# First stage over half of the rows for two sets of seven column tiles

## The chip, the cores and the metric

One core of one Trainium2 chip runs the kernel. The metric is device time in microseconds, the median of several runs. The engines are TensorE (matrix products into PSUM), VectorE, ScalarE, GpSimd and SyncE, which here issues every DMA. Each has its own queue of instructions; the kernel writes them in an order of its own (a manual schedule), and semaphores hold an instruction until its inputs and its buffer are ready. [...]

## The reference, cut to what matters

A layer over 512 latent tokens and 256 context tokens, 2048 wide:

```python
mod = silu(c) @ w_ada + b_ada            # c for latent, c_ctx for context; thirds: shift, scale, gate
h   = rmsnorm(x) * (1 + scale) + shift   # latent and context
b, c, u, g, v, q = split(h @ w_in)       # six parts of 1024 columns, 48 column tiles of 128
ya  = b * conv3(c * u) * silu(g)         # latent only
xb  = conv4(v) + bias                    # latent and context
for d in (forward, backward):            # RG-LRU, 16 heads of 64 channels
    r, i = sigmoid(xb @ wa + ba), sigmoid(xb @ wx + bx)
    a    = exp(-8 r softplus(-lam));  bt = sqrt(1 - a*a) * (i * xb)
    y   += linear_scan(a, bt)            # starts from the context's last state
yb  = y * silu(q)
out = rmsnorm(x + gate * (concat(ya, yb) @ w_out)) * final_g
```

## The kernel before, in words

Everything is fp32. A product is made of three passes in a reduced fp32 form (`mm3`, lines 77 to 80): the weights and the activations are each split into a high and a low part, and high by high, low by high and high by low are summed in one PSUM bank. So each weight tile of 128x1024 is loaded as `raw`, cast by ScalarE to `whi` (line 73), and VectorE makes `wlo` from the difference (line 74). Five `raw` buffers and three each of `whi` and `wlo` turn round. The activations lie transposed, 16 row tiles of 128 features by 512 tokens.

*Head.* The 16 tiles of x are loaded, squared and summed over the features by a product with ones into one of four column strips of the array (lines 208 to 219). From the ninth on each is followed by a product of ones with ones that nothing reads. The sums are gathered, an inverse root is made with one Newton step, transposed, and copied to all partitions (`rinvB`).

*Ada.* For each of the 16 row tiles g, shift and scale of latent and context are products of silu(c) and silu(c_ctx) with `w_ada`. `ada(g, p)` multiplies a quarter p of the rows: four products at a time in four column strips of 32. The weights come in four DMAs of 512 KB to eight buffers `rada`. After p = 3 ScalarE copies the sums (`sada`, line 205), two transposes and a few small VectorE instructions (`ada_t`, `mods`, lines 239 to 244) turn them into scale and shift, and `h_lat(g)` makes the activations: `xhi` on VectorE (line 247), its high part on ScalarE (248), the low part `hlo` on VectorE (249).

*First stage* (`main_a`). For each row tile k in turn, seven column tiles (A_TILES) are multiplied into seven banks, with the weights `wa_` of 448 KB a row tile. Between them stand, in this order: after tile 0 the split of the next row's weights (`split_a(k+1)`) and the second half of ada(k+1); after tile 1 `ada_t(k+1)` and `h_lat(k+1)`; after tile 5 the first half of ada(k+2). In k = 0 a softplus of 24 small VectorE instructions (`softplus`) follows `h_lat(1)`. The context tiles are loaded in the last two row tiles, squared by ScalarE after them and summed by GpSimd (`ctx_sq`).

*Steps.* The other 41 column tiles take two steps each, one for each half of the 16 row tiles, 24 products a step, with one weight piece of 512 KB a step, loaded three steps and split two steps ahead (`load_piece`, `split_piece`). BC_TILES sets the order: three tiles, the eight v tiles, which multiply the 256 context tokens too, the rest of c, u, b and g, and the eight q tiles. At the end of a step stands the evaluation (`EV`) of the tile that ended in the step before it, and then what the table `bg` says for the step; `mid` is issued between the fourth and the fifth row tile. The tables hold: the context's norm and activations (`ctx_stat`, `ctx_stat2`, `h_ctx`, steps 2 to 5); the gate third of ada as a sum on VectorE, one weight row of 512 KB every second step (`gt_load`, `gt_acc`), and at its end four sums over partitions (`gt_sum`); and from step S_C0 = 22 on the RG-LRU, one head tile m of 128 channels every seven steps. With b its first step: split of its weights and of xb (`l_prep`) at b, four gates (`l_gate`) in the middles of b+2 to b+5, tanh and exp (`l_exp`) at b+5, GpSimd and VectorE products (`l_mul`) at b+6, square roots (`l_sqrt`) at b+7, the scans (`l_scan`) at b+8. All gates use one pair of banks, which ScalarE's two sigmoids (`lr`, `li`, lines 460 and 461) free. `lr` and `li` have two buffers each, one a direction, which the scan of the head tile before still uses.

*Output.* 32 steps: four groups of 512 output columns by eight pieces of `w_out`. Each piece is multiplied with the gate first (VectorE, line 316) and then split; TensorE sums into four banks, one for each 128 tokens; `d_ev` adds x, squares and sums. The last pieces are reordered so that the final norm of each 128 tokens can start early.

Of the kernel before, what the change touches and what calls it, by code (L numbers as in the profile page):

```python
# [14 lines left out]
D = 2048  # L15
KT = D // 128
T = 512
# [12 lines left out]
for _n, _w in PCOLS:  # L30
# [5 lines left out]
A_TILES = [("c", 0), ("u", 0), ("b", 0), ("g", 0), ("c", 1), ("u", 1), ("b", 1)]  # L36
_REST = [("g", 1)] + [(n, m) for m in range(2, NM) for n in "cubg"]
N_FIRST = 3
BC_TILES = (_REST[:N_FIRST] + [("v", m) for m in range(NM)] + _REST[N_FIRST:]
            + [("q", m) for m in range(NM)])  # L40
NA = len(A_TILES)
W_OFF = {"b": 0, "c": 8, "u": 16, "g": 24, "v": 32, "q": 40}
N_BC = 2 * len(BC_TILES)
# [6 lines left out]
def tile_hybrid_layer(ctx, tc, xt, ct, xn, wada, wgt, bgt, wa_, wbc, wout, lruw, par, ident, fg, out):  # L50
# [11 lines left out]
    ctx.enter_context(tc.manual_schedule())  # L62
    s_a = ExitStack()
    ta = s_a.enter_context(tc.tile_pool(name="ta", bufs=2))
    pa = ctx.enter_context(tc.tile_pool(name="pa", bufs=6, space=PSUM))
# [96 lines left out]
    aux = pa.tile([128, 512], F32, name="bacc")  # L162
    acc = [pa.tile([128, 512], F32, name="bacc") for i in range(NA - 2)]
    accp = pa.tile([128, 2, 512], F32, name="plru", bufs=1)
    acc += [accp[:, 0, :], accp[:, 1, :]]
# [22 lines left out]
    for p in range(4):  # L188
        load_ada(0, p)
    load_wa(0)  # L190
    for p in range(4):
        load_ada(1, p)
    load_wa(1)

# [4 lines left out]
    def ada(g, p):  # L199
        for j in range(4):  # L200
            nc.tensor.matmul(aux[32 * j:32 * j + 32, 0:256], cs[:, 4 * p + j, :], rawa[g, p][:, j, :],  # L201
                             start=p == 0, stop=p == 3, skip_group_check=True)
        if p == 3:
            st = ta.tile([128, 256], F32, name="sada")
            nc.scalar.copy(st, aux[:, 0:256])
            rawa["s", g] = st
# [12 lines left out]
    ssum = ta.tile([128, T], F32, name="sq", bufs=4)  # L219
# [7 lines left out]
    ada(0, 0)  # L227
    ada(0, 1)
# [4 lines left out]
    ada(0, 2)  # L233
    ada(0, 3)

    def ada_t(g):
        st = rawa["s", g]
        for h in range(2):
            nc.tensor.transpose(aux[:, 256 + 128 * h:384 + 128 * h], st[:, 128 * h:128 * h + 128], idt)
        m = ta.tile([128, 2, 2], F32, name="mods")  # L240
        v = aux[:, 256:512].rearrange("p (s q v) -> p s v q", s=2, q=4)[:, :, 0:2, :]
        nc.vector.tensor_reduce(m, v, axis=AX.X, op=ALU.add)  # L242
        nc.vector.tensor_scalar(gs[:, g, :], m[:, 0, :], bsc1[:, g:g + 1], pc("ng", g), op0=ALU.add, op1=ALU.mult)
        nc.vector.tensor_scalar(sh[:, g, :], m[:, 1, :], pc("bsh", g), None, op0=ALU.add)
# [13 lines left out]
    def h_ctx(ks):  # L258
        for k in ks:
            nc.vector.scalar_tensor_tensor(xc[k], xc[k], gs[:, k, 1:2], cq["b"], op0=ALU.mult, op1=ALU.mult)  # L260
        for k in ks:
            hctx[k] = (hc.tile([128, TC], F32R, name="xchi", bufs=16 + NHC), hc.tile([128, TC], F32R, name="hclo"))
            nc.scalar.activation(hctx[k][0], xc[k], AF.Identity, bias=sh[:, k, 1:2])
        for k in ks:
# [3 lines left out]
    def ctx_sq(k):  # L268
        t = ta.tile([128, TC], F32, name="sqc", bufs=12) if k else const.tile([128, TC], F32, name="sqc0")
# [6 lines left out]
    def ctx_stat():  # L276
        ps = pa.tile([128, 512], F32, name="bacc")
# [7 lines left out]
    def ctx_stat2():  # L285
        ps = pa.tile([128, 512], F32, name="bacc")
# [5 lines left out]
    def main_a(k, j):  # L292
        hi, lo = wsp["a", k]
        s = slice(128 * j, 128 * j + 128)
        mm3(acc[j], hi[:, s], lo[:, s], hlat[k], T, k == 0, k == KT - 1)


    def piece_src(s):
        if s < N_BC:
            return wbc[s]  # L300
        return wout[s - N_BC]

# [7 lines left out]
    def split_piece(s):  # L310
        raw = rawq.pop(s)
        if s >= N_BC:
            c = (s - N_BC) // 8
# [5 lines left out]
    ada_t(0)  # L319
    h_lat(0)  # L320
    split_a(0)
    ada(1, 0)
    ada(1, 1)
    for k in range(KT):
        if k + 2 < KT:
            for p in range(4):
                load_ada(k + 2, p)
            load_wa(k + 2)
        else:
            load_piece(k + 2 - KT)  # L330
            for kk in range(8 * (k - 14), 8 * (k - 14) + 8):
                load_xc(kk)
        main_a(k, 0)
        if k + 1 < KT:
            split_a(k + 1)
            ada(k + 1, 2)
            ada(k + 1, 3)
        else:
            split_piece(0)
        main_a(k, 1)  # L340
        if k + 1 < KT:
            ada_t(k + 1)
# [12 lines left out]
    s_a.close()


    yp = ctx.enter_context(tc.tile_pool(name="yp", bufs=8, reuse_waits="tile"))
    gp = ctx.enter_context(tc.tile_pool(name="gp", bufs=1, reuse_waits="tile"))
    s_c = ExitStack()  # L360
    tq = [s_c.enter_context(tc.tile_pool(name="tcx", bufs=1, reuse_waits="tile"))]
    s_l = ExitStack()
    lp = [None]
    gacc = gp.tile([128, D], F32, name="gacc")
    nc.gpsimd.memset(gacc, 0.0)
# [12 lines left out]
    def ev_u(m, ps):  # L378
        cu = tq[0].tile([128, T], F32, name="cutile")
        nc.vector.tensor_tensor(cu, cur["c"], ps, op=ALU.mult)  # L380
        y = yp.tile([128, T], F32, name="yA")
# [30 lines left out]
    def ev_v(m, ps, psc):  # L412
        t = yp.tile([128, TA], F32, name="xb")
# [31 lines left out]
    def l_gate(m, d, h):  # L445
# [5 lines left out]
        ps = pa.tile([128, 2, 512], F32, name="plru", bufs=1)  # L451
        pf = ps.rearrange("p a b -> p (a b)")
# [53 lines left out]
    def gt_sum(j):  # L506
        p = pa.tile([128, 512], F32, name="bacc")
        s = slice(512 * j, 512 * j + 512)
        nc.tensor.matmul(p, ones, gacc[:, s], start=True, stop=True)
        nc.scalar.copy(gacc[:, s], p)  # L510
        gq[0] = gacc

    S_C0 = 2 * (N_FIRST + NM)
    bg, mid = {}, {}

    def at(step, f, *args, q=bg):
        q.setdefault(step, []).append((f, args))


    for m in range(NM):  # L520
        b = S_C0 + 7 * m
        if m:
            at(b, l_sqrt, m - 1)
        at(b, l_prep, m)
        if m:
            at(b + 1, l_scan, m - 1)
# [8 lines left out]
    at(S_C0 + 7 * NM, l_sqrt, NM - 1)  # L535
    at(S_C0 + 7 * NM + 1, l_scan, NM - 1)
    for i in range(N_GT):
        at(3 + 2 * i, gt_load, i)
        at(4 + 2 * i, gt_acc, i)
    for j in range(4):  # L540
        at(3 + 2 * N_GT + j, gt_sum, j)
    at(1, lambda: nc.sync.dma_start(gacc[0:1, :], bgt))
    at(2, ctx_stat)
    at(3, ctx_stat2)
    at(3, h_ctx, range(0, 3))
    at(4, h_ctx, range(3, 6))
    at(4, h_ctx, range(6, 9))
    at(5, h_ctx, range(9, 12))
    at(5, h_ctx, range(12, 15))
    at(5, h_ctx, range(15, 16))  # L550


    S_Y = S_C0 + 7 * NM + 2
# [8 lines left out]
    for k in range(6):  # L562
        at(S_Y + k // 3, lambda k=k: y_split(dp1[0], k))
# [230 lines left out]
```

## Time and profile before

| | us |
|---|---|
| median of 3 runs (857.98 to 859.2) | 858.03 |
| the profiled execution's own time | 858.19 |
| its span, first to last instruction | 856.4 |
| TensorE busy, of the span | 838.6 (98%) |
| VectorE, ScalarE, GpSimd busy | 493.5, 376.6, 89.1 |
| the 16th row tile of the first stage starts; the last of its products starts | 146.38; 150.91 |
| spacing of products in a step there | 0.227, so 24 take 5.45 |
| a v step (24 products of 512 and 24 of 256 columns) | 8.3 |
| VectorE: split of a piece; one gate row; gate on a piece of w_out | 1.25; 1.33; 1.30 |
| VectorE: the convolutions of one v tile | 4.8 |
| bytes moved, mean rate | 136.13 MB, 159 GB/s |

The profile is that of one execution. A busy TensorE says little, since its products are pipelined and the ends of the records are modelled: the spacing of starts counts. What matters is who waits: the chain of waits follows the execution back from its end, and the list of waits says which instruction an engine stood before and which other one released it. Lines are those of the kernel before.

### The profile page before, as it was taken

How to read it: one execution, taken by the hardware profiler on the slowest of the kernel's cores; microseconds unless marked ns; L12 is line 12 of the kernel's file. 1: busy time of each engine (PE TensorE's matmuls, PEld its weight loads, DVE VectorE, ACT ScalarE, POOL GpSimd, SP SyncE). 2: the span in 40 equal slices, each digit the busy share in tenths (PEclk: the TensorE clock that was granted, in tenths of full speed). 3: DMA queues.
4: the chain of work that ended last, by engine and by line, in shares of the span. 5: the costliest groups of instructions: out<-in, count | busy, mean ns of one | idle time of the engine just before them, and what ended most of it. 6: DMA issues, size and time to landing. Idle time of an engine off the chain costs nothing.

```text
span 856.4 us, 10577 instructions
## 1 busy us (share of the span) xinstructions
PE 838.6 (98%) x4202; PEld 665.3 (78%) x4202; DVE 493.5 (58%) x643; ACT 376.6 (44%) x478; POOL 89.1 (10%) x64
## 2 busy tenths in 40 slices
PE   7899999999999999999999999999999999999996
PEld 1466666888888888878888888887788888888784
DVE  0353434786355446394939585766465777454555
ACT  6322224451111024757576857475846443222234
POOL 0000001600000000202020202120202002020200
PEclk9899999999999999999999999999999999999998
DMA  9899998234222324244435443434223542323204
GB/s 341 341 326 333 352 357 291 103 120 139 82 99 82 116 86 159 99 131 152 143 116 164 145 159 122 161 123 135 74 99 141 204 171 102 120 74 113 84 0 197
DMA packets 41091, 136.13 MB, mean 159 GB/s; under 512 B 4561, under 2 KB 6865, under 8 KB 40401
## 3 DMA queue, kind: packets, MB, share of 16 engines
q1 hardware_dynamic: 41042, 135.46, 44.8%
q8 instruction: 33, 0.54, 0.3%
q14 instruction: 16, 0.13, 0.0%
HBM read 131.24 MB, written 4.19 MB: 158 GB/s over the span
## 4 chain that ended last, share of the span: by engine, by line
PE 93%; DVE 3%; ACT 1%; DMA 1%; issue 1%; SPq 0%; POOL 0%; ACTq 0%; DVEq 0%; POOLq 0%
PE bacc L78 21%; PE bacc L79 20%; PE bacc L80 20%; PE bacc L706 6%; PE bacc L708 6%; PE bacc L707 6%; PE bacc L201 4%; PE plru L78 1%; DMA xhi<-in_xt 1%; PE plru L454 1%; PE plru L79 1%; PE plru L80 1%; PE plru L706 1%; PE plru L708 1%; PE plru L707 1%; PE plru L456 1%
## 5 line engine op out<-in xcount | busy, mean ns | idle before, releaser
L78 PE MATMUL bacc<-xhi,whi 128*128 128x512 f32 x736 | 293.3, 399 | 1.6 <-ACT whi L73 1.6
L74 DVE TENSOR_TENSOR wlo<-raw,whi 128x1024 fp32r<-128x1024 f32 (+1 forms) x130 | 162.2, 1252 | 220.5 <-ACT whi L73 219.3
L79 PE MATMUL bacc<-xhi,wlo 128*128 128x512 f32 x736 | 288.1, 391 | 0.5 <-DVE wlo L74 0.5
L80 PE MATMUL bacc<-hlo,whi 128*128 128x512 f32 x736 | 287.7, 391 | 0.0
L73 ACT CAST whi<-raw 128x1024 fp32r<-128x1024 f32 (+1 forms) x130 | 134.3, 1035 | 246.3 <-PE bacc L80 127.2
L78 PEld LDWEIGHTS bacc<-xhi,whi 128*128 128x128 f32 x736 | 138.5, 188 | 37.2 <-issue 7.5
L80 PEld LDWEIGHTS bacc<-hlo,whi 128*128 128x128 f32 x736 | 138.6, 188 | 30.3
L79 PEld LDWEIGHTS bacc<-xhi,wlo 128*128 128x128 f32 x736 | 138.7, 188 | 28.3 <-DVE wlo L74 1.2
L706 PE MATMUL bacc<-whi,yhi 128*128 128x512 f32 x224 | 87.3, 390 | 0.3 <-DVE xr L639 0.3
L707 PE MATMUL bacc<-wlo,yhi 128*128 128x512 f32 x224 | 87.2, 389 | 0.0
L708 PE MATMUL bacc<-whi,ylo 128*128 128x512 f32 x224 | 87.1, 389 | 0.0
L464 POOL TENSOR_TENSOR li<-li,xb 128x768 f32<-128x768 f32 x16 | 30.9, 1933 | 393.5 <-ACT li L461 393.5
L460 ACT ACTIVATE lr<-plru,pt 64x768 f32<-64x768 f32 x32 | 28.8, 899 | 48.6 <-PE plru L457 41.7
L706 PEld LDWEIGHTS bacc<-whi,yhi 128*128 128x128 f32 x224 | 42.0, 188 | 9.4 <-DVE xr L639 0.8
L708 PEld LDWEIGHTS bacc<-whi,ylo 128*128 128x128 f32 x224 | 42.0, 188 | 8.8
L707 PEld LDWEIGHTS bacc<-wlo,yhi 128*128 128x128 f32 x224 | 42.0, 188 | 8.7
L504 DVE SCALAR_TENSOR_TENSOR gacc<-raw,cs,gacc 128x1024 f32<-128x1024 f32 x32 | 42.5, 1329 | 0.1
L316 DVE TENSOR_TENSOR raw<-raw,gacc 128x1024 f32<-128x1024 f32 x32 | 41.7, 1304 | 0.0
L80 PE MATMUL bacc<-hclo,whi 128*128 128x256 f32 x128 | 36.2, 283 | 0.0
L79 PE MATMUL bacc<-xchi,wlo 128*128 128x256 f32 x128 | 36.2, 283 | 0.0
L78 PE MATMUL bacc<-xchi,whi 128*128 128x256 f32 x128 | 36.1, 282 | 0.0
L201 PE MATMUL bacc<-rada,cs 128*32 128x256 f32 x512 | 35.1, 393 | 0.3 <-DVE mods L242 0.3
(158 smaller groups left out, 859.0 us busy)
## 6 DMA issues: line engine op xcount, KB each, us to landing
raw<-in_wbc SPq DMA_DIRECT2D x82, 512.0 KB, 3.2
rada<-in_wada SPq DMA_DIRECT2D x64, 512.0 KB, 5.7
raw<-in_wgt SPq DMA_DIRECT2D x32, 512.0 KB, 4.3
raw<-in_wout SPq DMA_DIRECT2D x32, 512.0 KB, 3.2
raw<-in_wa_ SPq DMA_DIRECT2D x16, 448.0 KB, 6.9
xhi<-in_xt SPq DMA_DIRECT2D x16, 256.0 KB, 4.9
xr<-in_xn SPq DMA_DIRECT2D x4, 1024.0 KB, 7.2
xchi<-in_ct SPq DMA_DIRECT2D x16, 128.0 KB, 3.7
```

What stands on the lines that cost most here:

```text
L73: nc.scalar.copy(hi[:, :n], raw[:, :n])
L74: nc.vector.tensor_tensor(lo[:, :n], raw[:, :n], hi[:, :n].bitcast(F32), op=ALU.subtract)
L78: nc.tensor.matmul(acc, wh, h[0][:, :n], start=first, stop=False, **kw)
L79: nc.tensor.matmul(acc, wl, h[0][:, :n], start=False, stop=False, **kw)
L80: nc.tensor.matmul(acc, wh, h[1][:, :n], start=False, stop=last, **kw)
L201: nc.tensor.matmul(aux[32 * j:32 * j + 32, 0:256], cs[:, 4 * p + j, :], rawa[g, p][:, j, :], start=p == 0, stop=p == 3, skip_group_check=True)
L316: nc.vector.tensor_tensor(r3, r3, g, op=ALU.mult)
L464: nc.gpsimd.tensor_tensor(lru["i", d], lru["i", d], xb[m], op=ALU.mult)
L504: nc.vector.scalar_tensor_tensor(gacc[:, s], gtq.pop(i), cs[:, k, 0:1], gacc[:, s], op0=ALU.mult, op1=ALU.add)
L706: nc.tensor.matmul(accs[t], yh[:, ts], hi[:, w], start=kk == 0, stop=False)
L707: nc.tensor.matmul(accs[t], yh[:, ts], lo[:, w], start=False, stop=False)
L708: nc.tensor.matmul(accs[t], yl[:, ts], hi[:, w], start=False, stop=kk == KT - 1)
```

## The change

The first stage covers only the first eight row tiles for seven column tiles (P_TILES). Their sums are copied from PSUM to SBUF (`part`). Then seven other column tiles (Q_TILES) start in the steps, first all their first halves and then all their second halves; ada(9) to ada(15) stand within the first seven of these steps. The second halves of the P tiles come later as single steps, in an order written out by hand, and their evaluation adds the stored part first (`ev_part`). In the diff KH is 8, `warm(n)` makes n products of ones with ones, `main_p` is `main_a` with the copy to `part` at k = 7, and the part with `s < NA` stands in the loop over the steps s, where k counts its eight row tiles. Now there are 89 steps; S_V = 14 is the first of the v tiles and S_C0 = 30.

```diff
-A_TILES = [("c", 0), ("u", 0), ("b", 0), ("g", 0), ("c", 1), ("u", 1), ("b", 1)]
+P_TILES = [("c", 0), ("u", 0), ("b", 0), ("g", 0), ("c", 1), ("u", 1), ("b", 1)]
+Q_TILES = [("c", 2), ("u", 2), ("b", 2), ("g", 2), ("c", 3), ("u", 3), ("b", 3)]
+def _order(names):
...
+    return [(t, h) for t in ts for h in range(t in P_TILES, 2)]
+STEPS = ([(t, 0) for t in Q_TILES] + [(t, 1) for t in Q_TILES]
+         + _order("v0 v1 v2 v3 v4 v5 v6 v7 c0 u0 c4 u4 b0 g0 b4 g4 c1 u1 c5 u5 b1 g1 g3 b5 g5"
+                  " c6 u6 b6 g6 c7 u7 b7 g7 q0 q1 q2 q3 q4 q5 q6 q7"))
...
-        t = ta.tile([128, 4, 256], F32, name="rada", bufs=8)
+        t = ta.tile([128, 8, 256], F32, name="rada", bufs=4)
...
+    def ada(g):
+        for p in range(4):
+            r = rawa[g, p // 2]
+            for j in range(4):
+                nc.tensor.matmul(aux[32 * j:32 * j + 32, 0:256], cs[:, 4 * p + j, :], r[:, 4 * (p % 2) + j, :],
+                                 start=p == 0, stop=p == 3, skip_group_check=True)
+        st = ta.tile([128, 256], F32, name="sada")
+        nc.scalar.copy(st, aux[:, 0:256])
...
-        sq = ta.tile([128, T], F32, name="sq", bufs=4)
-        nc.scalar.activation(sq, xl[k], AF.Square)
+        sq = ya.tile([128, T], F32, name="yA")
+        if k % 2:
+            nc.vector.tensor_tensor(sq, xl[k], xl[k], op=ALU.mult)
+        else:
+            nc.scalar.activation(sq, xl[k], AF.Square)
...
-        if k >= 8:
-            nc.tensor.matmul(acc[0][:, :128], ones, ones, start=True, stop=True)
+    warm(3)
...
-    ada(0, 0)
-    ada(0, 1)
+    ada(0)
+    ada_t(0)
...
-    ada(0, 2)
-    ada(0, 3)
+    warm(8)
...
+    def h_ada(k):
+        ada(k)
+        if k + 2 < KT:
+            for p in range(2):
+                load_ada(k + 2, p)
...
+    for k in range(KH):
+        if k + 2 < KH:
             load_wa(k + 2)
         else:
+            load_piece(k + 2 - KH)
+        main_p(k, 0)
+        h_ada(k + 1)
+        if k + 1 < KH:
             split_a(k + 1)
         else:
             split_piece(0)
+        main_p(k, 1)
+        ada_t(k + 1)
+        h_lat(k + 1)
         if k == 0:
             softplus()
+        for j in range(2, NA):
+            main_p(k, j)
...
+    S_L = [S_C0 + b for b in (0, 7, 14, 21, 28, 35, 41, 47)]
+    for m, b in enumerate(S_L):
+        tight = m + 1 < NM and S_L[m + 1] < b + 7
         at(b, l_prep, m)
         for i in range(4):
             at(b + 2 + i, l_gate, m, i // 2, i % 2, q=mid)
...
+        at(b + 7, l_sqrt, m, first=True)
+        at(b + 7 if tight else b + 8, l_scan, m)
     for i in range(N_GT):
-        at(3 + 2 * i, gt_load, i)
-        at(4 + 2 * i, gt_acc, i)
-    for j in range(4):
-        at(3 + 2 * N_GT + j, gt_sum, j)
+        at(S_V + i // 2, gt_load, i)
+        at(S_V + 1 + i // 2, gt_acc, i)
+    for j in range(2):
+        at(S_V + 4 + N_GT // 2 + j, gt_sum, 2 * j)
...
+    def ev_part(n, m, ps):
+        t = part[P_TILES.index((n, m))]
+        nc.vector.tensor_tensor(t, t, ps, op=ALU.add)
+        if n == "c":
+            cur["c"] = t
+        else:
+            EV[n](m, t)
...
+            if s < NA and k == 2:
+                h_ada(KH + 1 + s)
+            if s < NA and k == 4:
+                ada_t(KH + 1 + s)
+                h_lat(KH + 1 + s)
...
+        if c < 3:
+            g = dp1[0].tile([128, T], F32, name="sgt", bufs=1)
+            nc.vector.tensor_tensor(g, gq[0][:, s], ps, op=ALU.mult)
+            ps = g
```

Beside this: three context squares share a tile and stand in steps 7 to 9, the context's norm and activations in steps 10 to 14; `gt_sum` makes two sums at a time; the PSUM banks are named, six in turn and the pair, and the output stage alternates between two full sets of four; the gate is multiplied into the last eight pieces of `w_out` only; the six first splits of y stand two a step.

## Rows read from the trace of the kernel before

**Rows 1.** The page, part 4: chain that ended last, by engine.

```profile
PE 93%; DVE 3%; ACT 1%; DMA 1%; issue 1%; SPq 0%; POOL 0%; ACTq 0%; DVEq 0%; POOLq 0%
```

**Rows 2.** Waits of TensorE, 130 to 850 us: us in total, times, longest.

```profile
PE plru L454 <- ACT li L461: 0.5, 1, 0.5
PE bacc L706 <- DVE xr L639: 0.3, 1, 0.3
```

**Rows 3.** Chain that ended last, the head: start us, us, what.

```profile
28.01 0.38 ACT sada L205
...
29.61 0.67 DVE xhi L247
```

**Rows 4.** Windows: engines' busy us (instructions), granted clock, DMA share, GB/s.

```profile
0.00:8.00 8.00, 3.83 (x9) 0.79 (x10) 0.73 (x5) 4.43 (x6) 0.20 (x4) 1.00 0.75 238
8.00:13.00 5.00, 4.76 (x15) 0.96 (x12) 0.00 (x0) 4.05 (x7) 0.00 (x0) 1.00 1.03 388
13.00:23.00 10.00, 9.45 (x27) 2.85 (x28) 0.35 (x4) 5.12 (x8) 0.00 (x0) 1.00 1.03 409
...
30.00:32.00 2.00, 0.38 (x9) 0.10 (x1) 1.14 (x3) 1.70 (x3) 0.00 (x0) 1.00 0.96 350
32.00:35.00 3.00, 2.52 (x11) 0.99 (x15) 1.98 (x2) 0.69 (x1) 0.00 (x0) 0.52 1.03 406
```

**Rows 5.** Timeline of TensorE: start us, us, line, out<-in [idle before <-releaser].

```profile
31.90 0.65 PE L78 MATMUL bacc<-xhi,whi 128*128 128x512 f32 x1 [1.62 <-ACT whi L73]
...
38.78 0.46 PE L80 MATMUL bacc<-hlo,whi 128*128 128x512 f32 x1
...
51.33 1.07 PE L201 MATMUL bacc<-rada,cs 128*32 128x256 f32 x16
52.33 0.50 PE L78 MATMUL bacc<-xhi,whi 128*128 128x512 f32 x1
...
58.79 1.07 PE L201 MATMUL bacc<-rada,cs 128*32 128x256 f32 x16
```

**Rows 6.** Timeline of ScalarE in one row tile of the first stage.

```profile
52.46 0.37 ACT L205 COPY sada<-bacc 128x256 f32<-128x256 f32 x1 [1.75 <-PE bacc L201]
55.00 0.72 ACT L248 ACTIVATE xhi<-xhi,sh 128x512 fp32r<-128x512 f32 x1 [2.16 <-DVE xhi L247]
55.63 0.92 ACT L73 CAST whi<-raw 128x896 fp32r<-128x896 f32 x1
```

**Rows 7.** Timeline of VectorE in the same row tile.

```profile
53.62 0.17 DVE L242 TENSOR_REDUCE mods<-bacc 128x4 f32<-128x16 f32 x1 [1.78 <-PE bacc L239]
...
55.76 0.75 DVE L249 SCALAR_TENSOR_TENSOR hlo<-xhi,sh 128x512 fp32r<-128x512 f32 x1 [0.85 <-ACT xhi L248]
56.58 1.09 DVE L74 TENSOR_TENSOR wlo<-raw,whi 128x896 fp32r<-128x896 f32 x1
```

**Rows 8.** Timeline of VectorE: first and last of the softplus.

```profile
42.00 0.17 DVE L147 TENSOR_SCALAR w<-w 128x16 f32<-128x16 f32 x1 [0.88 <-ACT w L146]
...
46.76 0.17 DVE L159 TENSOR_SCALAR nsp<-w 128x16 f32<-128x16 f32 x1
```

**Rows 9.** Timeline of TensorE: last gate of head tile 6, second of 7.

```profile
599.42 0.39 PE L454 MATMUL plru<-xs,lwh 128*128 128x512 f32 x1
...
630.09 0.50 PE L454 MATMUL plru<-xs,lwh 128*128 128x512 f32 x1
```

**Rows 10.** Timeline of VectorE between these two gates.

```profile
614.44 0.96 DVE L477 SCALAR_TENSOR_TENSOR lt<-lx,lt 128x768 f32<-128x768 f32 x1 [1.65 <-POOL lx L476]
...
617.55 1.94 DVE L441 TENSOR_TENSOR xs<-xb,xs 64x768 fp32r<-64x768 f32 x2
...
622.73 0.95 DVE L486 TENSOR_TENSOR lt<-lt,li 128x768 f32<-128x768 f32 x1
...
628.41 0.69 DVE L492 TENSOR_TENSOR xb<-li 128x512 f32<-128x512 f32 x1
```

**Rows 11.** Groups by line and form, 370 to 800 us: VectorE, evaluation of u.

```profile
L387 DVE SCALAR_TENSOR_TENSOR yA<-cutile,pt,yA 128x504 f32<-128x504 f32 x5 | 3.7, 744 | 0.2
```

More of the change, by code (lines that the diff above doesn't have):

```diff
@@ L62, in tile_hybrid_layer, with bank @@
     ctx.enter_context(tc.manual_schedule())
+    ya = ctx.enter_context(tc.tile_pool(name="ya", bufs=9))
     s_a = ExitStack()
     ta = s_a.enter_context(tc.tile_pool(name="ta", bufs=2))
-    pa = ctx.enter_context(tc.tile_pool(name="pa", bufs=6, space=PSUM))
+    pa = ctx.enter_context(tc.tile_pool(name="pa", bufs=1, space=PSUM))
+    single = [pa.tile([128, 512], F32, name=f"bank{i}") for i in range(6)]
+    pair = pa.tile([128, 2, 512], F32, name="pair")
+    turn = [5]
+    def bank():
+        turn[0] += 1
+        return single[(turn[0] - 1) % 6]
     def raw_tile():
@@ L159, in softplus @@
         nc.vector.tensor_scalar(nsp8, w0, -LRU_C, None, op0=ALU.mult)
[L162 to L165, printed above, removed]
+    aux = single[5]
+    acc = single[:5] + [pair[:, 0, :], pair[:, 1, :]]
     cq = {}
@@ L186, in split_a @@
         wsp["a", k] = split(rawq.pop(("a", k)), NA * 128)
-    for p in range(4):
+    for p in range(2):
         load_ada(0, p)
     load_wa(0)
-    for p in range(4):
+    for p in range(2):
         load_ada(1, p)
     load_wa(1)
+    for p in range(2):
+        load_ada(2, p)
     gs = const.tile([128, KT, 2], F32, name="gs")
@@ L276, in ctx_stat @@
     def ctx_stat():
-        ps = pa.tile([128, 512], F32, name="bacc")
+        ps = bank()
         for j in range(2):
@@ L285, in ctx_stat2 @@
     def ctx_stat2():
-        ps = pa.tile([128, 512], F32, name="bacc")
+        ps = bank()
         for j in range(2):
@@ L506, in gt_sum, with at @@
     def gt_sum(j):
[L507 to L510, printed above, removed]
+        ps = [bank() for _ in range(2)]
+        for i in range(2):
+            nc.tensor.matmul(ps[i], ones, gacc[:, 512 * (j + i):512 * (j + i) + 512], start=True, stop=True)
+        for i in range(2):
+            nc.scalar.copy(gacc[:, 512 * (j + i):512 * (j + i) + 512], ps[i])
         gq[0] = gacc
-    S_C0 = 2 * (N_FIRST + NM)
+    S_C0 = S_V + 2 * NM
     bg, mid = {}, {}
[L516 to L523, printed above, removed]
+    def at(step, f, *args, q=bg, first=False):
+        t = q.setdefault(step, [])
+        t.insert(0 if first else len(t), (f, args))
+    S_L = [S_C0 + b for b in (0, 7, 14, 21, 28, 35, 41, 47)]
+    for m, b in enumerate(S_L):
+        tight = m + 1 < NM and S_L[m + 1] < b + 7
         at(b, l_prep, m)
-        if m:
-            at(b + 1, l_scan, m - 1)
         for i in range(4):
@@ L583, in tile_hybrid_layer @@
     load_piece(2)
-    for s in range(N_BC):
-        ti, half = divmod(s, 2)
-        n, m = BC_TILES[ti]
+    for s, ((n, m), half) in enumerate(STEPS):
+        if s in (NA - 2, NA - 1):
+            for k in range(8):
+                load_xc(8 * (s - NA + 2) + k)
+        if s == NA:
+            s_a.close()
+            xbp = ctx.enter_context(tc.tile_pool(name="xbp", bufs=8, reuse_waits="tile"))
+            gp = ctx.enter_context(tc.tile_pool(name="gp", bufs=1, reuse_waits="tile"))
+            tq[0] = s_c.enter_context(tc.tile_pool(name="tcx", bufs=1, reuse_waits="tile"))
+            gacc = gp.tile([128, D], F32, name="gacc")
+            nc.gpsimd.memset(gacc, 0.0)
         if s + 3 < NS:
@@ L596, in tile_hybrid_layer @@
             split_piece(s + 2)
-        for _ in range(min(len(evq), 4 if s == 0 else 2)):
-            evq.pop(0)()
         hi, lo = wsp.pop(s)
-        if half == 0:
-            accs[ti] = [pa.tile([128, 512], F32, name="bacc")]
-            if n == "v":
-                accs[ti].append(pa.tile([128, 512], F32, name="bacc"))
-        for k in range(8):
+        t = (n, m)
+        if t in Q_TILES:
+            accs[t] = [acc[Q_TILES.index(t)]]
+        elif t not in accs:
+            accs[t] = [bank(), bank()] if n == "v" else [bank()]
+        new = half == 0 or t in P_TILES
+        for k in range(KH):
             if k == 4:
@@ L691, in tile_hybrid_layer @@
                     d_ev(pend[0], t, pend[1][t])
-            accs = [pa.tile([128, 512], F32, name="bacc") for _ in range(2 if c == 1 else 4)]
-            if c == 1:
-                pp = pa.tile([128, 2, 512], F32, name="plru", bufs=1)
-                accs += [pp[:, 0, :], pp[:, 1, :]]
+            if c < 2:
+                sets = (sets if c else []) + [[bank() for _ in range(2 if c else 4)]]
+                if c == 1:
+                    sets[1] += [pair[:, 0, :], pair[:, 1, :]]
+            accs = sets[c % 2]
         if q < 5:
```

169 lines of the change are left out of this document (71 added, 98 removed).

## The prediction

> **What bounds the kernel now.** First the chain of waits: 93% of it is TensorE [rows 1]. Then who made TensorE wait after the first stage: two waits in 720 us, 0.5 us for ScalarE's `li` and 0.3 us for a bank in the output stage [rows 2]. So past 130 us time comes only from fewer TensorE cycles or is lost by new waits. The changed kernel multiplies the same products (48 column tiles by 16 rows by 3, eight tiles of context, 32 gates, 32 output pieces), so what can move is the head, the ada batches between the products of the first stage, and waits.
>
> The head ends at 31.90 us, when the first product starts behind `whi` [rows 5]. Until about 23 us it is a row of square sums with warm-up products between them, while the input queue runs at 388 to 409 GB/s [rows 4]. [...]
>
> In the first stage one row tile takes 7.46 us (58.79 less 51.33, [rows 5]): 21 products, two half batches of ada matmuls, two transposes. ScalarE and VectorE hold 2 us of slack there: `hlo` of the next row ends at 56.51 [rows 7], and the row needs it after 58.
>
> **The change, part by part.** I follow TensorE to the point where 82 weight steps are left. That is 151.1 us before (the 16th row starts at 146.4, 21 products of 0.227). Afterwards it is the start of the step numbered 7.
>
> *Start.* The squares are shared by ScalarE and VectorE, and the warm-ups between the sums go. Then ada(0) is bound by its transfer: 4.36 MB of inputs and 2.10 MB of ada weights. The windows carry 1.90 MB to 8 us, 3.84 to 13, and 0.409 MB a us after [rows 4], so 6.46 MB have moved at 19.4; with 1 us for landing (estimate, 0 to 2) and 1.1 for the second half of the batch, ada(0) ends at 21.5. The sum of squares is not later (last x tile at 15.3 by the same count, then an estimated 5 us for its sum, the copy and the Newton step). From ada(0)'s copy to `xhi` it was 1.60 (28.01 to 29.61, [rows 3]), here some 0.65 more, as the four transposes of the inverse norm now stand behind; from `xhi` to the first product 2.29 (29.61 to 31.90, [rows 3, 5]). First product at 26.1 instead of 31.9: -5.8 (bounds -4.5 and -6.9). But half of ada(1) was done in the old head: +1.2.
>
> *Clock.* At the lower level the first nine products, 16 ada matmuls and two transposes took 6.9 us (31.90 to 38.78, [rows 5]); at upper-level durations, with the wait for `wlo`, 4.4. So 2.5 us come back if the clock stays up. In the new head eight warm-up products fill TensorE until about 25 us; idle are then 1.1 us to the first product and 0.9 to the second. Before, TensorE was busy 0.38 us of the 2 us to 32 us when the clock fell [rows 4]. Bounds 0 and -2.5; I take -2.5, since the idle stretch before that fall (1.6 of 2 us, with thin work ahead of it) was longer than either gap, and keep the rest as a rival. [...]
>
> *One batch in place of two.* A half batch takes 1.00 us (51.33 to 52.33, [rows 5]), 0.86 of it streaming (four groups of 0.215) and 0.14 drain; 0.09 stand ahead and some 0.14 behind, where the next three products run at 0.24. A batch of 32 is 0.86 longer than one of 16 and saves one of the switches: 0.37 a row, 7.09 instead of 7.46. Fifteen times: -5.6 (bounds -2.8, -7).
>
> *What that batch does to ScalarE.* Before, the split of the next weights (`whi`, `wlo`) was issued ahead of ada's copy and ran while TensorE multiplied [rows 6, 7]. Now `h_ada(k+1)` is issued ahead of `split_a(k+1)`, so `whi` stands behind `sada` on ScalarE, and `wlo` ahead of the modulation on VectorE. That the engines keep this order although they idle is seen at 55.00: ScalarE sat 2.16 us before `xhi` with the cast for the next weights, whose data had long come, behind it [rows 6]. From the end of the batch: `sada` from 0.13 to 0.50, `whi` 0.92 to 1.40, `wlo` 1.09 to 2.52, then the stretch from `mods` to the end of `hlo`, 2.89 (53.62 to 56.51, [rows 7]): 5.35. The third product of the next row needs it; then 0.32 to the next batch and 1.86 for it: a loop of 7.55 us a row, 0.46 over TensorE's 7.09. Seven rows: +3.2. In the first of them `softplus` puts 24 small instructions (42.00 to 46.93, [rows 8]) on VectorE ahead of the next `wlo`; before they ran in slack, now half of them are in the loop: +1.9 (bounds 0 and +4.9). Together +5.1 (0 to +8).
>
> *Two sets.* The seven Q tiles take the rest of ada in their steps. Its copy and transposes stand two products apart there, and `h_lat(8+s)` isn't needed until step 7: no wait. The queue needs 2.62 MB in 7.8 us, 336 GB/s, and it did 409 [rows 4]. The partial sums are copied while TensorE is in other banks. Sum to this point: -5.8 + 1.2 - 2.5 - 5.6 + 5.1 = -7.6.
>
> *Gate sum in the v steps, batched context.* Two gate rows a v step: VectorE has 1.2 for `wlo`, 2.6 for two rows and some 2.4 for the convolution in a step of 8.3 us. That cover holds by 2 us; SP, which loads the next piece behind those rows, is three steps ahead. Context tiles the same: 0.
>
> *LRU heads.* Here is the price. From the last gate of head tile 6 (599.42) to the second gate of tile 7 (630.09) TensorE has five steps, 30.7 us [rows 9], and even so the answer came when it was due: `lt` ends at 615.40, VectorE does the next tile's split (`xs`) and `wlo`, then starts the scan at 622.73, ends it at 629.10 [rows 10]; `li` (0.9) frees the bank pair. In the new plan tiles 5 and 6 start the next one after six steps, not seven: the blocked gate comes four steps later, 4 x 5.45 + 2 x 0.71 = 23.2 us after the last. The scan now is issued one step earlier, but the rows before it stay: `lt` at 15.3 to 16 after the gate, 0.7 for `lwl`, 1.94 for `xs`, 1.2 for `wlo`: scan from 19 to 25.4, `li` to 26.3. Wait 3.1 at tile 6 to 7; at 5 to 6, where no sigmoid stands in that stretch, 1.7. At tile 0 to 1, where the old wait of 0.5 was, the mixed order puts u4's four VectorE instructions (0.74 or less each, [rows 11]) ahead of `l_mul` and b0's two behind it, against one gate row of 1.3 that left: wait 2.7, part of it for u4's bank. Tile 1 to 2: 1.0. Sum 8.5, bounds 2 (if only the tight pair shows, half) and 12; less the 0.5 of before, +8.0. The rest of the heads have less on VectorE than before: 0.
>
> *Output stage.* Three of four column groups lose 1.3 us a piece of VectorE work, hidden before as now; two full sets of banks take away the wait of 0.3 [rows 2]: -0.3. The tail is the same.
>
> Sum: -7.6 + 8.0 - 0.3 = +0.1. The profiled execution took 858.19 us with a span of 856.4; its own time is 0.16 above the median of 858.03. Forecast 858.2: no change, as two effects of eight microseconds cancel.
>
> **Rivals.** *The clock falls again* before the first products. For it: the two gaps, and the fall of before in a like place. Against: the eight warm-ups end 1 us ahead of the first product. It decides when the granted clock shows the lower level between 26 and 33 us; price 1.6 (one batch and a few products at half speed) to 2.5: 860.2, slower. *The LRU waits stay away*, because sqrt and scan in one step are early enough: for it, the new steps carry no gate rows, so VectorE may get to the scan sooner than I reckon; against, the row at 622.73, where the scan waited for VectorE's queue and not for its input. Then -7.6 - 0.8: about 850. *The first stage does not wait*: if `whi` of the next row gets ahead or the loop has slack, 5.1 us less: 853.
>
> **How the numbers follow.** Forecast 0.42 (own range 856 to 860.5), clock 0.28, no LRU waits 0.15, no waits in the first stage 0.15. A change within 0.2% (1.7 us) can't be told from none. Faster: most of the last two (0.27) and 0.07 of the forecast's lower end: 0.34. Slower: 0.21 of the clock's case and 0.07 of the forecast's upper end: 0.28. Same: 0.38. Range 852 to 862: it leaves out most of the case at 850 and sums of both losses.
>
> **What would show it.** First product near 26 us; ada in 16 batches of 32; TensorE waiting for `hlo` at each of rows 1 to 7 and longest at row 2; the step with 82 left near 143.5. In the LRU stage TensorE waiting for `li` at four places, 1 to 3 us each, longest at head tile 7. Wrong if those waits are missing while the head is as said (then near 850), or if the steps of v or the context wait, for which I charged nothing.

## The result and the profile after

The changed kernel takes 865.99 us (median of 7, 861.80 to 867.87), the kernel before 857.98 (median of 7, 857.12 to 859.2): ratio 1.0088, 95% interval 1.0067 to 1.0108. It is 0.9% slower; "no change" was wrong, and the time lies above the range. The profiled execution took 864.93 us with a span of 863.1, 6.7 more than before.

First the chain of waits of the changed kernel, by engine (page, part 4; answers to [rows 1]):

```profile
PE 78%; DVE 10%; ACT 7%; DMA 2%; issue 2%; POOL 1%; SPq 0%; ACTq 0%; POOLq 0%; DVEq 0%
```

TensorE's share fell from 93% to 78%: the end now hangs for longer on VectorE and ScalarE. Who made TensorE wait, without the waits of the head (total us, times, longest; answers to [rows 2]):

```profile
PE pair L478 <- ACT li L485: 7.4, 4, 3.0
...
PE pair L97 <- DVE yA L363: 3.4, 1, 3.4
PE bank L97 <- ACT xhi L274: 1.8, 1, 1.8
...
PE bank L97 <- DVE cutile L405: 0.8, 1, 0.8
PE pair L752 <- DVE xr L684: 0.8, 1, 0.8
```

The line on `yA` (copies of the partial sums) and the last one (output stage) stand in no step of the prediction. Next TensorE's timeline (start us, us, line, [idle before <-releaser]; answers to [rows 5]): the first product, the ada batches, the two waits, the first product of step 7.

```profile
26.06 0.50 PE L97 MATMUL bank<-xhi,whi 128*128 128x512 f32 x1 [1.26 <-ACT whi L92]
...
27.85 3.21 PE L223 MATMUL bank<-rada,cs 128*32 128x256 f32 x32
...
36.74 1.94 PE L223 MATMUL bank<-rada,cs 128*32 128x256 f32 x32
...
45.05 0.51 PE L97 MATMUL bank<-xhi,whi 128*128 128x512 f32 x1 [1.82 <-ACT xhi L274]
...
46.57 3.02 PE L223 MATMUL bank<-rada,cs 128*32 128x256 f32 x32
...
62.91 1.94 PE L223 MATMUL bank<-rada,cs 128*32 128x256 f32 x32
70.53 1.94 PE L223 MATMUL bank<-rada,cs 128*32 128x256 f32 x32
...
91.19 0.39 PE L99 MATMUL pair<-hlo,whi 128*128 128x512 f32 x1
94.99 0.50 PE L97 MATMUL pair<-xhi,whi 128*128 128x512 f32 x1 [3.41 <-DVE yA L363]
...
150.28 0.39 PE L97 MATMUL bank<-xhi,whi 128*128 128x512 f32 x1
```

Two batches of the same 32 matmuls took 3.21 and 3.02 us, all others 1.93 or 1.94: the clock was down. The windows (engines' busy us, granted clock, DMA share, GB/s; answers to [rows 4]) show it at its lower level (0.50 of full speed) twice, each time behind an idle stretch:

```profile
27.00:28.00 1.00, 0.81 (x6) 0.45 (x10) 0.14 (x1) 0.00 (x0) 0.00 (x0) 1.00 1.02 420
...
29.00:30.00 1.00, 1.00 (x15) 0.45 (x11) 0.00 (x0) 0.00 (x0) 0.00 (x0) 0.50 1.02 426
...
44.00:45.00 1.00, 0.00 (x0) 0.00 (x0) 0.24 (x1) 0.72 (x1) 0.00 (x0) 1.00 0.94 392
...
47.00:48.00 1.00, 1.00 (x16) 0.54 (x12) 0.00 (x0) 0.00 (x0) 0.00 (x0) 0.50 0.06 16
```

The mark that the prediction set, the step with 82 steps left, comes at 150.28; 143.5 was forecast, 151.1 it was before. Behind it there are 863.1 - 150.3 = 712.8 us; forecast were 713.0. So the whole miss, 6.8 us, lies ahead of the mark. It is made of three things:

| first stage | forecast | measured |
|---|---|---|
| first product | 26.1 | 26.06 |
| row period | 7.55 | 7.62 (70.53 less 62.91): +0.5 over seven rows |
| wait behind softplus | 1.9 | 1.82 |
| copies of the partial sums | 0 | 94.99 less 91.19, less the usual 0.23: +3.6 |
| clock | stays up | two falls: 1.3 (first product to second batch 10.68, with the clock up 9.42) and 1.4 (from there to the fourth batch 18.55, with the clock up 17.16): +2.7 |

The times with the clock up are those of the run copy_last below, which is the same kernel up to the eighth row:

```profile
25.64 0.49 PE L97 MATMUL bank<-xhi,whi 128*128 128x512 f32 x1 [1.26 <-ACT whi L92]
...
35.06 1.93 PE L223 MATMUL bank<-rada,cs 128*32 128x256 f32 x32
...
52.22 1.93 PE L223 MATMUL bank<-rada,cs 128*32 128x256 f32 x32
```

The changed kernel's fourth batch starts at 55.29. 0.5, 3.6 and 2.7 make 6.8, the whole miss.

The copy of `pair` on VectorE, which TensorE waited for, stands behind the modulation and the next row's `h`:

```profile
91.39 0.75 DVE L273 SCALAR_TENSOR_TENSOR xhi<-xhi,gs,rinvB 128x512 f32<-128x512 f32 x1
92.98 0.75 DVE L275 SCALAR_TENSOR_TENSOR hlo<-xhi,sh 128x512 fp32r<-128x512 f32 x1 [0.85 <-ACT xhi L274]
93.65 0.68 DVE L363 COPY yA<-bank 128x512 f32<-128x512 f32 x1
94.25 0.68 DVE L363 COPY yA<-pair 128x512 f32<-128x512 f32 x1
```

The sixth tile lies in the first half of the bank pair, the seventh in the second; both halves are one tile of the program. TensorE had finished the sixth and wanted to write the seventh into the other bank, and had to wait until the sixth was read.

### The profile page after: what moved, and what is told of

It is laid out like the page before. It is cut to its first block, busy times and chain, and to the rows that moved or that the text cites. A ratio compares the mean times of both kernels' runs of the same rounds, so it can differ in the third digit from the quotient of the medians.

```text
span 863.1 us, 10486 instructions
## 1 busy us (share of the span) xinstructions
PE 831.9 (96%) x4208; PEld 666.3 (77%) x4208; DVE 480.2 (56%) x648; ACT 373.0 (43%) x471; POOL 87.6 (10%) x64
## 4 chain that ended last, share of the span: by engine, by line
PE 78%; DVE 10%; ACT 7%; DMA 2%; issue 2%; POOL 1%; SPq 0%; ACTq 0%; POOLq 0%; DVEq 0%
PE bank L99 16%; PE bank L97 16%; PE bank L98 16%; PE bank L754 5%; PE bank L752 5%; PE bank L753 5%; PE bank L223 3%; DVE wlo L93 2%; PE pair L752 2%; PE pair L754 2%; PE pair L753 2%; ACT whi L92 1%; DMA rada<-in_wada 1%; DMA xhi<-in_xt 1%; PE pair L97 1%
## 5 line engine op out<-in xcount | busy, mean ns | idle before, releaser
L97 PE MATMUL bank<-xhi,whi 128*128 128x512 f32 x720 | 286.0, 397 | 3.9 <-ACT xhi L274 1.8
L99 PE MATMUL bank<-hlo,whi 128*128 128x512 f32 x720 | 282.1, 392 | 0.3
L98 PE MATMUL bank<-xhi,wlo 128*128 128x512 f32 x720 | 281.1, 390 | 0.6 <-DVE wlo L93 0.6
L97 PEld LDWEIGHTS bank<-xhi,whi 128*128 128x128 f32 x720 | 135.3, 188 | 39.4 <-issue 7.2
L99 PEld LDWEIGHTS bank<-hlo,whi 128*128 128x128 f32 x720 | 135.3, 188 | 32.3 <-DVE hlo L275 3.2
L98 PEld LDWEIGHTS bank<-xhi,wlo 128*128 128x128 f32 x720 | 135.5, 188 | 26.9 <-DVE wlo L93 0.9
L752 PE MATMUL bank<-whi,yhi 128*128 128x512 f32 x192 | 74.7, 389 | 0.0
L754 PE MATMUL bank<-whi,ylo 128*128 128x512 f32 x192 | 74.7, 389 | 0.0
L753 PE MATMUL bank<-wlo,yhi 128*128 128x512 f32 x192 | 74.7, 389 | 0.0
L753 PEld LDWEIGHTS bank<-wlo,yhi 128*128 128x128 f32 x192 | 36.1, 188 | 7.5
```

The source lines that it names most:

```text
L97: nc.tensor.matmul(acc, wh, h[0][:, :n], start=first, stop=False, **kw)
L98: nc.tensor.matmul(acc, wl, h[0][:, :n], start=False, stop=False, **kw)
L99: nc.tensor.matmul(acc, wh, h[1][:, :n], start=False, stop=last, **kw)
L752: nc.tensor.matmul(accs[t], yh[:, ts], hi[:, w], start=kk == 0, stop=False)
L753: nc.tensor.matmul(accs[t], yh[:, ts], lo[:, w], start=False, stop=False)
L754: nc.tensor.matmul(accs[t], yl[:, ts], hi[:, w], start=False, stop=kk == KT - 1)
```

## The experiments

All are edits of the changed kernel. "Before" ran beside each group at 857.8 to 858.1.

**copy_last.** The sixth copy behind the seventh tile's products:

```diff
-            if j % 2:
-                nc.vector.tensor_copy(part[j], acc[j])
-            else:
-                nc.scalar.copy(part[j], acc[j])
+            for i in (j,) if j < 5 else () if j == 5 else (5, 6):
+                if i % 2:
+                    nc.vector.tensor_copy(part[i], acc[i])
+                else:
+                    nc.scalar.copy(part[i], acc[i])
```

> Only change: in the eighth row of the first stage the copy of the sixth partial sum (first half of the bank pair) is issued behind the seventh tile's products instead of ahead of them. Theory 1 (the two halves of the pair are one tile, so the seventh tile's products wait for VectorE's copy of the sixth, which stands behind the modulation and h of the next row): the wait of 3.4 us of the product on `pair` for VectorE's `yA` at 91 to 95 us goes, nothing takes its place, 3.4 us less: near 862.5. Rival 1 (the copies as such are too slow, and the first Q tile then waits for a bank or for a weight split instead): another wait of 2 to 3.5 us stands between 92 and 98 us, time near 866. If the gap also let the clock fall in some executions, the spread of the times narrows too.

Median 861.12 (860.69 to 863.75). TensorE's waits from 80 to 105 us hold a single line:

```profile
PE bank L232 <- ACT sada L226: 0.7, 1, 0.7
```

The wait of 3.4 is gone and 0.7 took its place. Theory 1 holds: with the same engines, the same copies and the same banks, only the order against the other half of the pair decided. The spread of the times narrowed as well, from 6.1 to 3.1 us.

**split_first.** The next weights' split ahead of the ada batch:

```diff
-        h_ada(k + 1)
         if k + 1 < KH:
             split_a(k + 1)
         else:
             split_piece(0)
+        h_ada(k + 1)
```

> Only change: in the first stage the split of the next row's weights is issued ahead of the ada batch and its copy, as in the kernel before. Theory 1 (the split stands behind the batch's copy on ScalarE and makes the loop 0.46 us a row longer than TensorE's work): row period from 7.62 to 7.1 to 7.2 us, the weight loads' wait for `hlo` (3.2 us in 7) gone; the wait of 1.8 behind softplus stays, since VectorE still runs softplus first: 3 us less, near 863. Rival 1 (the row is bound by the copy of the batch and what follows it, not by the split): period stays at 7.6, time near 866. A wait of 3.4 for the copy of the partial sum at 91 us stays under both, within 1 us.

Median 860.85 (858.33 to 861.77). The ada batches show the row period:

```profile
52.83 1.93 PE L223 MATMUL bank<-rada,cs 128*32 128x256 f32 x32
59.92 1.93 PE L223 MATMUL bank<-rada,cs 128*32 128x256 f32 x32
```

7.09 us, the figure that the prediction worked out for TensorE's own work with one batch a row (before: 7.46, [rows 5]). The waits at softplus (1.3) and at the copy (1.8) shrank as well, since VectorE gets to them earlier; that is why it gained 5.1 in place of the expected 3. That the copy's wait would stay near 3.4 was a miss: 1.6 of it came with the order of the split.

**soft_late.** Softplus in the second tile set:

```diff
-        if k == 0:
-            softplus()
...
+        if s == 1:
+            softplus()
```

> Only change: softplus is issued in the second step of the second tile set instead of in the first row of the first stage. Theory 1 (softplus on VectorE delays the second row's h by 1.8 us, and this idle stretch is what lets the clock fall a second time): the wait of 1.82 at 43 us goes and the granted clock stays at the upper level from 42 to 50 us: 1.8 + 1.6 = 3.4 us less, near 862.5. Rival 1 (the clock's fall at 45 us does not hang on that gap): the wait goes but the lower level shows again somewhere between 36 and 60 us: 1.8 less, near 864. Rival 2 (softplus only moves its cost): TensorE waits 1 to 2 us in the second tile set, time near 866.

Median 864.4 (862.05 to 864.83). The wait behind softplus is gone and none came in its place in the second set. The clock stayed up from 24 to 60 us, but fell at two later places, where it had not fallen in the profile of the changed kernel: behind the copy's wait, at 90 us, and behind a wait of 3.0 us for `li` ahead of a gate of head tile 7:

```profile
627.37 0.79 PE L476 MATMUL pair<-xs,lwh 128*128 128x512 f32 x1 [3.00 <-ACT li L483]
...
628.81 0.63 PE L97 MATMUL bank<-xhi,whi 128*128 128x512 f32 x1
```

Products take 0.63 us at the lower level, else 0.39 or 0.40. The gain of 1.6 is about the wait's alone, the size that rival 1 gave; but the fall between 36 and 60 us that was to go with it did not show. For theory 1's second half one profile is too little.

**lrli3.** Three buffers for the gates' results:

```diff
-            lru["r", d] = lp[0].tile([128, TA], F32, name="lr", bufs=2)
-            lru["i", d] = lp[0].tile([128, TA], F32, name="li", bufs=2)
+            lru["r", d] = lp[0].tile([128, TA], F32, name="lr", bufs=3)
+            lru["i", d] = lp[0].tile([128, TA], F32, name="li", bufs=3)
...
-            x = lp[0].tile([128, TA], F32, name="lx")
+            x = lp[0].tile([128, TA], F32R, name=f"xs{d}").bitcast(F32)
```

> Only change: three buffers instead of two for the gates' results `lr` and `li` (room for them by putting the squares `lx` into the tiles `xs`, which are idle by then). Theory 1 (the next head's first sigmoids write the buffers that the scan of the head before still reads, so gate 2 waits through ScalarE for VectorE's scan): all four waits of TensorE for `li` (7.4 us together) go, near 858.5. Rival 1 (the place of the work in ScalarE's and VectorE's queues is the cause, not the buffers: sigmoids stand behind the square roots, and the split of the next head's input behind the previous tile's work): waits of 4 to 7 us stay at the same four places, 862 to 866. Rival 2 (the later square now waits for `xs`): new waits of the gates for `xs`, 1 to 2 us a head, over 866.

Median 856.62 (11 runs, 855.80 to 858.27), 9.4 less than the changed kernel; at one mean clock (0.991 of full speed over the execution) the spans are 855.8 to 856.2 against 864.2 to 864.3, 8.2 less. No wait on `li` is left among TensorE's. How the wait came about is seen in the changed kernel where it was longest (ScalarE, VectorE, TensorE):

```profile
626.49 1.28 ACT L484 ACT_TABLE_LOAD   x1 [4.74 <-DVE li L513]
627.79 0.90 ACT L484 ACTIVATE lr<-pair,pt 64x768 f32<-64x768 f32 x1
629.79 0.90 ACT L485 ACTIVATE li<-pair,pt 64x768 f32<-64x768 f32 x1 [1.11 <-DVE xb L516]
...
629.07 0.69 DVE L516 TENSOR_TENSOR xb<-li 128x512 f32<-128x512 f32 x1
...
630.74 0.50 PE L478 MATMUL pair<-xs,lwh 128*128 128x512 f32 x1 [3.00 <-ACT li L485]
```

The sigmoids of the next head idle until VectorE has done with the scan of the first direction (L513, which reads `lr`) and then with the sum `xb` (L516, which reads `li`): they write the buffers that these read. TensorE waits behind them for the pair. The edit did one thing more: the two squares have a tile each, so `l_mul`'s two parts need not follow one another through one `lx`. The next run leaves that out.

**li3.** The third buffer for `li` alone.

> Changed kernel with a third buffer for `li` alone, one look. Theory 1 (the last reader, the sum of the two scans, holds `li`; `lr` comes free at the end of the first direction's scan, 2.4 to 3.2 us earlier): TensorE's four waits shrink from 7.4 to about 1.5 to 2.5 and ScalarE's idle time ahead of the sigmoid L485 behind VectorE's `xb` is gone; what is left waits for `lr`. Rival 1 (`lr` decides alone): the waits stay at 7 or more.

One run, 861.25. TensorE's wait:

```profile
PE pair L478 <- ACT li L485: 2.3, 2, 1.9
```

5.1 of the 7.4 us hung on `li`'s buffer alone, as theory 1 has it. In this run ScalarE still waits 4.76 us at head tile 7 until L513 is done, ahead of the sigmoid that writes `lr`, and the one that writes `li` follows at once: what is left hangs on `lr`'s buffer. Whether the separate squares alone would have ended it was not run.

**even.** Seven steps between all head tiles:

```diff
-    S_L = [S_C0 + b for b in (0, 7, 14, 21, 28, 35, 41, 47)]
+    S_L = [S_C0 + b for b in (0, 7, 14, 21, 28, 35, 42, 49)]
...
-    S_Y = S_L[-1] + 9
+    S_Y = S_L[-1] + 8
...
-        at(S_Y + k // 2, lambda k=k: y_split(dp1[0], k))
+        at(S_Y + k // 3, lambda k=k: y_split(dp1[0], k))
```

> Only change to the changed kernel: the eight head tiles all start seven steps apart (0, 7, ... 42, 49 instead of ... 35, 41, 47); the six y splits follow in two steps instead of three. Theory 1 (two of the four waits come from the steps that were shortened to six, two from the mixed order around u4 and c5 and u1): the waits of 1.5 at 592 and 3.0 at 631 us go, those of 1.6 at 389 and 1.2 at 431 stay, TensorE waits 2.9 instead of 7.4 for `li`: near 861. Rival 1 (two buffers don't do at either spacing, as the scan stands behind the next tile's split anyway): a wait of 0.5 to 1.5 stays at heads 6 and 7, near 863. Rival 2 (later y splits now hold up the output stage): a wait of TensorE for `yhi` behind 700 us, no gain.

Median 861.34 (860.35 to 863.29). TensorE's waits behind 300 us:

```profile
PE pair L478 <- ACT li L485: 2.9, 2, 1.6
PE bank L754 <- DVE ylo L607: 1.6, 1, 1.6
```

Exactly the two of the shortened steps went (4.5 of 7.4); the two of the mixed order stayed. Rival 2 took 1.6 of it back: the splits of `y` now come too late for the output stage. Steps or buffers, either ends these two waits; but the steps are taken from the end, where the output stage needs them.

**tail_sum.** Two edits far apart, one run:

```diff
-        at(S_V + 4 + N_GT // 2 + j, gt_sum, 2 * j)
+        at(S_V + 1 + N_GT // 2 + j, gt_sum, 2 * j)
...
-                sets = (sets if c else []) + [[bank() for _ in range(2 if c else 4)]]
-                if c == 1:
-                    sets[1] += [pair[:, 0, :], pair[:, 1, :]]
+                sets = (sets if c else []) + [[bank() for _ in range(4 if c else 2)]]
+                if c == 0:
+                    sets[0] += [pair[:, 0, :], pair[:, 1, :]]
```

> Only two changes far apart, one look: the pair belongs to the first set of banks of the output stage instead of the second, and the gate sum stands three steps earlier. Theory 1 (in the last group the fourth token tile's products wait for VectorE's read of the third, as both lie in the pair; u4's bank comes late because the gate sum's copies stand on ScalarE ahead of `whi` and `wlo`, and those ahead of u0's product): the wait of 0.8 on `pair` for `xr` and the wait of 0.8 on a bank for `cutile` both go, 1.6 us less at the same clock. Rival 1: the last group ends with the same dependence, because VectorE is late at the end in any bank: a wait of 0.3 to 0.8 on a bank for `xr`. Rival 2: moved sums collide with the first head tile's split: another wait of 0.5 to 1 between 325 and 345 us.

865.07, mean clock 0.994. Both waits of 0.8 are gone, yet two others show:

```profile
PE pair L478 <- ACT li L485: 9.1, 4, 3.3
...
PE bank L533 <- DVE gacc L528: 0.5, 1, 0.5
```

The output stage's wait was the shared pair once more. The early gate sum gained nothing by itself: the wait of 0.8 for u4's bank went, but the gate behind it waited 3.32 instead of 1.64, and the sum 0.5 for the last gate row, together 1.3 us more. Both pairs of sums now stand ahead of head tile 0's last gate, which starts 2.3 us later (357.58 for 355.28), and its scan, which the waiting gate needs, 1.2 later. Rival 2 has the size and the place of the new wait (332.7 us), but not its cause: the sum waits for a gate row, not for a split.

**all_warm8, all_warm13.** All edits above in one (without `even`), with eight warm-ups, and with thirteen:

```diff
-    warm(8)
+    warm(13)
```

> All edits tried so far in one kernel (copy of the sixth partial sum behind the seventh tile, split ahead of the ada batch, softplus late, three buffers for `lr` and `li`), and two more: the output stage's first set of banks takes the pair, so that the last column group has single banks, and the gate sum stands three steps earlier; warm-ups as in the changed kernel. Theory 1 (each wait has a cause of its own and they add): from the profiled 864.9, less 8.1 for the head waits, 3.7 for seven rows at 7.09 instead of 7.62, 3.4 for the copy, 1.8 for softplus, 0.8 for the output stage, 0.8 for u4's bank, and about 1.6 for the one clock fall that then cannot happen: 844.7, range 843 to 847. Rival 1 (the waits cover for one another, so that one removed lets another show): two or more new waits over 1 us on TensorE between 30 and 850 us, 849 to 853. By theory 1 the only place left where the clock can fall is 26 to 33 us: executions at two levels some 1.6 us apart.

> As the run before, with thirteen warm-up products instead of eight ahead of the first product. Theory 1 (the idle 1.2 us ahead of the first product is what lets the clock fall in some executions): no execution shows the lower level at 26 to 33 us, mean clock the same in all; the median is that of the run before without falls, 0 to 1.6 us less. Rival 1 (the gap behind the first product, 0.6 us of waiting for `wlo`, or the thin ada products decide): falls as often as before, same times. Rival 2 (the warm-ups run past the point at which `whi` is ready): first product 0.2 to 0.5 us later and the time as much longer.

845.18 (844.18 to 846.05) and 845.25 (844.56 to 847.48). The sum of theory 1 was 844.7: the causes add, within a microsecond (the profiled execution of the kernel with eight, in which the clock did not fall before the end, took 844.3, with two small new waits, 1.0 for `sada` and 0.5 for `gacc`). Its four executions lie at two levels, 844.2 to 844.3 and twice 846.05, as expected. But five more warm-ups gained nothing here: two of five executions have a mean clock of 0.994, where none was expected to fall. The profile of one of these two says why, though only for one execution: the clock is up at 26 us and falls at another gap, 1.93 us for `sada`, whose copy stands on ScalarE behind a weight cast that waits for its transfer (ScalarE, then TensorE):

```profile
89.27 1.04 ACT L92 CAST whi<-raw 128x1024 fp32r<-128x1024 f32 x1 [2.72 <-DMA raw<-in_wbc]
90.22 0.37 ACT L226 COPY sada<-bank 128x256 f32<-128x256 f32 x1
...
90.64 0.44 PE L232 MATMUL bank<-idt,sada 128*128 128x128 f32 x2 [1.93 <-ACT sada L226]
...
92.04 0.63 PE L98 MATMUL bank<-xhi,wlo 128*128 128x512 f32 x1
```

Products take 0.63 us from 91.6 to 94.6. Now that the first stage is faster, the input queue is late at its end.

**late_t8, late_t13.** As these two, the transposes two row tiles later in the second set's steps, the gate sum one step later than there:

```diff
-            if s < NA and k == 4:
+            if s < NA and k == 6:
                 ada_t(KH + 1 + s)
...
-        at(S_V + 1 + N_GT // 2 + j, gt_sum, 2 * j)
+        at(S_V + 2 + N_GT // 2 + j, gt_sum, 2 * j)
```

> As all_warm8, with two edits: in the steps of the second tile set the transposes of ada stand two row tiles later (the copy `sada` there stands on ScalarE behind a weight cast that waits for its transfer), and the gate sum is issued one step later than there. Theory 1 (the only gap left for the clock to fall in, apart from the one at 26 us, is TensorE's wait for `sada` at 88 to 91 us): that wait (1.0, and 1.9 with thirteen warm-ups) goes or falls under 0.6, the wait of 0.5 for `gacc` too; 843 to 844.5, with the upper level from 86 to 100 us. Rival 1 (the late transfer of the weight piece takes its place: products wait for `wlo` or the next ada batch for its data): a wait of 0.5 to 1.5 between 90 and 105 us, 845.

> As the run before, with thirteen warm-ups instead of eight ahead of the first product. Theory 1 (with the later gap gone, the one at 26 us alone decides between the levels): all executions within 0.5 us and at one mean clock, while the run with eight shows two levels about 1.6 us apart. Rival 1 (falls come without a gap that the profile shows): executions at lower mean clock here as well, 1 to 2 us longer.

Eight warm-ups: 843.98 (843.81 to 845.0, mean clock of each execution 0.994 to 0.996). Thirteen: 843.04 (842.21 to 843.44, 0.997 to 0.998), against 858.11 of the kernel before, ratio 0.9823 (0.9809 to 0.9836). The window from 28 us in the two profiles, first with eight, then with thirteen:

```profile
28.00:30.00 2.00, 2.00 (x24) 0.95 (x20) 0.68 (x1) 0.94 (x1) 0.00 (x0) 0.50 1.00 418
```

```profile
28.00:30.00 2.00, 2.00 (x34) 1.12 (x27) 0.31 (x1) 1.21 (x2) 0.00 (x0) 1.00 1.03 428
```

With the later gaps gone, filling the one at 26 us keeps the mean clock at 0.997 or more in all four timed executions; that is theory 1 of late_t13, though they spread over 1.2 us and not 0.5. The two levels that it expected of late_t8 did not show: there the mean clock is lower in all five. This kernel is 1.8% faster than the one before. From 27 to 150 us, TensorE's waits in its profile are:

```profile
PE bank L98 <- DVE wlo L93: 0.6, 1, 0.6
PE bank L232 <- ACT sada L226: 0.4, 1, 0.4
```

## Why the prediction was wrong

*Where it was right.* The start (26.06 for 26.1; the 1 us for landing in it was an estimate that no row gives, but ada(0) ended at 21.65 for 21.5), the saving of one batch (row of 7.09 once nothing waits), the loop through ScalarE's order (7.62 for 7.55, and split_first shows that the order is its cause; its terms, 2.52 and 2.89, make 5.41 and not 5.35, so the loop should have been put at 7.6), softplus (1.82 for 1.9). The heads: at tile 0 to 1 1.64 and u4's bank 0.8 (forecast 2.7), then 1.2 (1.0), 1.5 (1.7), 3.0 (3.1); together 8.2 for 8.5, at the four places named. That context tiles and gate rows in the v steps cost nothing: no wait there.

*First failed step, 3.6 us: "The partial sums are copied while TensorE is in other banks".* I counted banks, but the program's dependences go by tiles, and two of the seven banks are one tile. I also did not ask what stood on VectorE ahead of that copy: the modulation and `h` of the next row. copy_last shows the first; the second is in VectorE's rows above and in split_first, where the wait shrank to 1.8. The banks of the sixth and the seventh tile did differ, and yet TensorE waited 3.41 us: in this program two banks that are one tile wait as one.

*Second failed step, 2.7 us in the profiled execution: "I take -2.5" for the clock.* This was my first rival, with a price of 1.6 to 2.5 for one fall ahead of 33 us. The fall there cost 1.3, but there was a second, behind the softplus wait, and there are four gaps where it can happen; the prediction weighed only the first. In the profiles of the changed kernel and of the experiments with eight warm-ups the clock fell at the first gap (1.3 and 0.6 us) in 6 of 10; at the softplus wait of 1.8 to 1.9 in 2 of 6; at the copy's wait of 3.4 in 4 of 6; and at the wait of 3.0 ahead of head tile 7's gate in 3 of 5. Against profiles in which the clock stayed up at the same place, a fall cost 1.3 to 1.6 us at the first gap, 1.3 and 1.4 at the second, 1.5 to 2.7 at the copy, 1.3 to 2.8 at the gate. Four such gaps can explain why the changed kernel's executions lie 6 us apart (861.80 at a mean clock of 0.997, 867.87 at 0.989) and those of before 2 us; it is not shown, since only one execution of each kernel has a profile, and the mean clock also counts the end, where TensorE is idle and the clock low (0.50 from 858.0 to 863.1 us in the changed kernel's profile, with TensorE busy for 0.00).

*Third, 0.8 us, hidden in a right sum: the output stage.* "Two full sets of banks take away the wait" was forecast at -0.3; the second set has the pair in it, and the wait grew from 0.3 to 0.8. At the back that is offset by the head waits, which came out 0.3 low, and by smaller items that I did not track.

So the loss of eight microseconds behind the mark came as forecast, but the gain ahead of it was 0.9 us (151.14 to 150.28) instead of 7.6, because the first stage lost 3.6 to a dependence that nothing in the mathematics asks for, 2.7 to the clock and 0.5 to a slightly longer row.

## What to carry to other kernels

Before a copy out of a bank is costed at nothing, ask which tile the bank belongs to, and what stands ahead of the copy on its engine: here the second half of a tile of two banks could be written only when the copy of the first half was done, and TensorE waited 3.41 us for it. Where a stage of the next round waits for a scan, look first for the buffer that both use; one more buffer for each of two results (room for it came from a tile that is idle by then) was worth 8 us; the one shift of steps that was tried removed 4.5 us of waits and brought 1.6 back. And short idle stretches of TensorE between its products (0.6 to 3.5 us here) had a price in the clock that differed from execution to execution, from none to 2.8 us a gap: give it as a chance for each gap, or fill the gap.

## What the runs showed of the hardware

After the same idle stretch the clock fell in one execution and not in the next: with 1.25 or 1.26 us of idle ahead of the first product and 0.62 or 0.63 behind it, the ada batch that follows took 1.93 us in 4 profiles of kernels with eight warm-ups and 3.01 to 3.50 in 6. No run shows what decides between the two. Nor was the longest of the four gaps a sure fall: ahead of the seventh tile's products TensorE sat idle for 3.4 or 3.5 us, and the clock stayed up in 2 of 6 profiles. And a fall had no one price: ahead of head tile 7's gate one fall cost 1.3 us and another 2.8.
